# Three small edits in a one-core hybrid attention block: where the norm weights are loaded, how far mixer A's heads are staged apart, how early the last splits are issued

## The chip, the cores and the metric

The kernel runs on one core of a Trainium2 chip. The metric is the device time of one execution in microseconds (us); lower is better. A core has a matrix engine (TensorE, PE in the rows; its weight loads are PEld), a vector engine (VectorE, DVE), a scalar engine (ScalarE, ACT), GpSimd (POOL) and SyncE (SP), which here only issues DMAs. Each engine works its own list of instructions in order and waits on semaphores for the others.

## The reference

One layer of a decoder trunk on x of 256 tokens by 4096 channels, all in float32:

```
h    = rmsnorm(x, norm_g)
proj = h @ w_in                       # 4096 x (26 chunks of 512, and 48 gate columns)
o_a  = dilated attention of 16 heads over q_a, k_a, v_a      (mixer A)
o_b  = compressed / selected / window attention, 16 heads    (mixer B)
y    = concat(rmsnorm(o_a) * silu(z_a), rmsnorm(o_b) * silu(z_b))
x    = rmsnorm(x + y @ w_out, final_g)
```

In mixer A the three patterns of a head act on one 256-token sequence, so the kernel computes one softmax per head with a table of multiplicities (`MULT`) and a table of distances (`DA`).

## The kernel before

Every float32 product is made of three fast products: an operand is split into a rounded part h and a rest l, and `mm3` (lines 98 to 100) adds h·h, h·l and l·h. `split_to` (lines 105 and 106) makes the two parts of a weight tile: ScalarE writes h, then VectorE writes l from it. So each weight tile passes through SyncE's queue (load), ScalarE, VectorE and TensorE, in this order.

The program has four parts. **Part one** streams three weight chunks past x (`run_stream`): `stage_unit` loads weight units `w`, `load_xT` loads the transposed x in pieces `xp`, `split_x` makes `xh` and `xl` = x times the norm weights `g_in`, and `split_unit` makes `wh` and `wl`. Every `xh` reads `g_in`. The first unit is loaded and split in small pieces so that TensorE can begin early; before that TensorE runs 13 dummy products (`warm_up`). **Part two** (`run_pairs`) computes most of the projection by a fast block scheme. **Part three** streams the z chunks and the first output chunk, and between their products the two attentions run: they are generators in a queue `tasks`, and `advance()` takes one step of the first of them, about 1.5 steps per 128 rows of weights. The attention of mixer A is `attend_a`, once for each group of four heads; its three stages per head are `scores` (products `s`, then the softmax numerators `n` on VectorE and ScalarE), `turn` (transposes `pt` of `n`, line 677, and the split `pah`, `pal`) and `values` (products `po`). `pipeline(units, stages, at)` runs them in rounds, where stage f of unit j comes in round j + at. `mixer_done` loads the stored z tiles (`sz`), applies silu and multiplies them into the output. **Part four** is `run_pairs` for the output projection and then two chunks of 256 columns. The last chunk is held back: its pieces are split into `ehl` and `eh`/`el` by `split_held` and kept, since all products for the first 128 tokens are done before those for the second 128.

A tile scheduler orders each engine's list in parts one and three by its own estimate; parts two and four stand as written. Each DMA that SyncE or ScalarE issues takes one of eight DMA semaphores in turn (DMAHW0 to 7), and an issue waits until the DMA that had this semaphore eight issues ago has landed.

Of the kernel before, what the change touches and what calls it, by code (L numbers as in the profile page):

```python
# [83 lines left out]
def hybrid_trunk(ctx: ExitStack, tc: tile.TileContext, a: dict):  # L84
    nc = tc.nc
# [32 lines left out]
    g_in = cst.tile([P, KT], F32, name="g_in")  # L118
# [13 lines left out]
    def load_xT(piece):  # L132
        q, half = divmod(piece, 2)
        if half == 0:
            xh.append(big.tile([P, QK, SEQ], F32R, name=f"xh{q}", tag="x", bufs=8))
            xl.append(big.tile([P, QK, SEQ], F32R, name=f"xl{q}", tag="x", bufs=8))
        t = x_raw[piece] = room["o"].tile([P, G4, SEQ], F32, name="xp", tag="o", bufs=8)
        if piece == 0:
            nc.gpsimd.dma_start(g_in, a["norm_g"])
            for j, e in ((0, 1), (1, 2), (2, 4)):  # L140
                nc.sync.dma_start(t[:, j:e], a["xT"][piece, :, j:e])
        elif piece == 1:
            for j in range(0, G4, 2):
                nc.sync.dma_start(t[:, j : j + 2], a["xT"][piece, :, j : j + 2])
        else:
            nc.sync.dma_start(t, a["xT"][piece])
# [10 lines left out]
    def load_x_nat(i):  # L157
        m, q = divmod(i, 4)
        t = x_nat[i] = room["work"].tile([P, DM // 4], F32, name="xn", tag="xn", bufs=4)
        nc.sync.dma_start(t, a["x"][m * P : (m + 1) * P, q * DM // 4 : (q + 1) * DM // 4])  # L160
# [109 lines left out]
            square_x(2 * (u - 8) + half)  # L270
        splitted[u, half] = (h, l)

    LOOK = 2
    def split_held(u, half, i):

        t = staged[u]
        n, width = 4, units[u][1]
        if i < 5:
            hl = room["held"].tile([P, 2, n, width], F32R, name="ehl", tag="ehl", bufs=5)
            h, l = hl[:, 0], hl[:, 1]  # L280
        else:
            h = room["split"].tile([P, n, width], F32R, name="eh", tag="wh")
            l = room["split"].tile([P, n, width], F32R, name="el", tag="wl")
        split_to(h, l, t[:, half * n : (half + 1) * n])
        splitted[u, half] = (h, l)
# [13 lines left out]
    def run_stream(begin=None, last=False, ordered=None):  # L299
        subs = [(u, s) for u in range(len(units)) for s in range(2)]  # L300
        n_st = n_sp = 0
        credit = 0.0
        ps = None
        first = room["first"]
        held_chunk = len(chunks) - 1 if last else None
        for i, (u, s) in enumerate(subs):
            while True:
                if n_st < len(units) and n_st <= u + (2 if i else 0):
                    if first and n_st < 8:
                        load_xT(n_st)  # L310
                    stage_unit(n_st)
                    if first and 8 <= n_st < 12:
                        load_x_nat(2 * (n_st - 8))
                        load_x_nat(2 * (n_st - 8) + 1)
                    n_st += 1
                    if first and n_st == 1:
                        warm_up()
                    if first and n_st == 6:
                        early_loads()
                elif n_sp < len(subs) and n_sp <= i + LOOK and subs[n_sp][0] < n_st:  # L320
                    if units[subs[n_sp][0]][4] == held_chunk:
                        if n_sp == len(subs) - 8:
                            open_held()
                        split_held(*subs[n_sp], n_sp - len(subs) + 8)
                    else:
                        split_unit(*subs[n_sp])
                    n_sp += 1
                elif i == 0 and n_st < 3:
                    if first:
                        load_xT(n_st)  # L330
                    stage_unit(n_st)
                    n_st += 1
                else:
                    break
            if i == 0 and begin:
                begin()
                if ordered:
                    ordered.close()
            src, width, k0, n, c = units[u]
            n //= 2  # L340
            _, lhs, done, before, pace = chunks[c]
            if k0 == 0 and s == 0:
                if before:
                    before()
                ps = [room["acc"].tile([P, CW], F32, name="acc", tag="acc") for _ in range(NT)]
            if c == held_chunk:
                wh, wl = splitted[u, s]
                for j in range(n):
                    h, l = lhs(k0 + n * s + j, 0)
                    mm3(ps[0][:, :width], h, l, wh[:, j], wl[:, j], start=(i == len(subs) - 8 and j == 0),  # L350
                        stop=(i == len(subs) - 1 and j == n - 1))
                for _ in range(2):
                    advance()
                continue
            wh, wl = splitted.pop((u, s))
            for j in range(n):
                k = k0 + n * s + j
                for m in range(NT):
                    h, l = lhs(k, m)
                    mm3(ps[m][:, :width], h, l, wh[:, j], wl[:, j], start=(k == 0), stop=(k == KT - 1))  # L360
                if k == KT - 1:
                    done(ps)
                if (c, k) in hooks:
                    hooks[c, k]()
                credit = min(credit + pace * width / CW, 2.0)
                while credit >= 1.0 and tasks:
                    credit -= 1.0
                    advance()
        if not last:
            return  # L370

        while tasks:
            advance()
        done(ps, 0)
        for i, (u, s) in enumerate(subs[-8:]):
            wh, wl = splitted.pop((u, s))
            k0, n = units[u][2:4]
            n //= 2
            for j in range(n):
                h, l = lhs(k0 + n * s + j, 1)  # L380
                mm3(ps[1][:, :width], h, l, wh[:, j], wl[:, j], start=(i == 0 and j == 0), stop=(i == 7 and j == n - 1))
        done(ps, 1)
# [241 lines left out]
    def pipeline(units, stages, at):  # L624

        for t in range(len(units) + at[-1]):
            for f, d in reversed(list(zip(stages, at))):
                if 0 <= t - d < len(units):
                    f(units[t - d])
            yield  # L630
            yield

    def attend_a(hg):
# [59 lines left out]
                nc.scalar.activation(t[:, m], po[:, m], AF.Copy, scale=rden[:, m : m + 1])  # L693
            nc.vector.tensor_add(o_at("a", head * HD, HD), t[:, :, 0], t[:, :, 1])

        yield from pipeline(range(4), [scores, turn, values], [0, 1, 2])
        square_sums("a", hg)

    def square_sums(which, hg):
# [520 lines left out]
    def early_loads():  # L1220
        nc.sync.dma_start(ident, a["consts"][:, N_CONST - P :])
        nc.sync.dma_start(g_out, a["out_g"])
# [231 lines left out]
```

## Time and profile before

| | |
|---|---|
| median of three runs | 1630.84 us (1629.99 to 1634.46) |
| profiled execution, its own time | 1628.41 us |
| its span, first to last instruction | 1626.6 us |
| TensorE busy | 1605.9 us, 99% of the span |
| VectorE, ScalarE busy | 1369.2 us, 995.5 us |
| mean granted TensorE clock | 0.998 of full speed |

The span is what the trace shows; the profiled execution's own time has 1.8 us more around it. TensorE is busy nearly all the time, so what can be read from the trace is above all where it is not.

### The profile page before, as it was taken

The page shows a single profiled execution, that of the slowest core. Times are in us where ns is not written, and L with a number is a line of the kernel's source. Part 1 is how long each engine was busy: PE and PEld are TensorE (multiplying, and loading weights), DVE is VectorE, ACT ScalarE, POOL GpSimd, SP SyncE. Part 2 cuts the span into 40 slices and gives each one's busy share as a digit, 9 for nine tenths or more (in the row PEclk, how much of TensorE's full clock was granted, in tenths as well). Part 3 has the DMA queues.
Part 4 walks back from the last instruction along what each step waited for, and adds up shares of the span by engine and source line. Part 5 has one row for each costly group of instructions (what it writes and reads, how often), then busy time and mean ns, then how long its engine had stood idle before and what let it go on. Part 6 is the DMA issues. An engine that isn't in the chain of part 4 may idle for free.

```text
span 1626.6 us, 20699 instructions
## 1 busy us (share of the span) xinstructions
PE 1605.9 (99%) x7685; PEld 1324.3 (81%) x7685; DVE 1369.2 (84%) x1596; ACT 995.5 (61%) x1242; POOL 143.3 (9%) x197
## 2 busy tenths in 40 slices
PE   8999999999999999999999999999999999999997
PEld 6998888888888888888887777888888888888896
DVE  7679989898999898989878788888777769989884
ACT  7755656565656565656546666766667655656553
POOL 0000212020212021202000000000000000212110
PEclk9999999999999999999999999999999999999999
DMA  8776888888888788978787464643355456878874
GB/s 326 275 249 209 259 264 256 256 260 264 255 269 263 247 265 259 269 242 269 242 333 300 157 213 170 227 140 127 135 187 182 170 200 212 261 250 257 279 300 166
DMA packets 104452, 384.86 MB, mean 237 GB/s; under 512 B 12368, under 2 KB 13024, under 8 KB 92960
## 3 DMA queue, kind: packets, MB, share of 16 engines
q1 hardware_dynamic: 81648, 332.40, 57.9%
q0 software_dynamic: 22272, 50.10, 13.8%
q8 instruction: 60, 0.98, 0.2%
q10 hardware_dynamic: 432, 1.05, 0.2%
q14 instruction: 40, 0.33, 0.1%
HBM read 334.69 MB, written 50.91 MB: 237 GB/s over the span
## 4 chain that ended last, share of the span: by engine, by line
PE 84%; DVE 7%; DMA 4%; issue 2%; ACT 2%; POOL 0%; SPq 0%; ACTq 0%; POOLq 0%; DVEq 0%
PE p L99 15%; PE p L100 15%; PE p L98 15%; PE acc L99 8%; PE acc L100 8%; PE acc L98 8%; PE e L100 2%; PE e L99 2%; PE e L98 2%; DVE bf L440 1%; DMA bw<-in_w_in 1%; DVE bf L439 1%; PE ph L872 1%; PE pt L1053 1%; DVE bt L433 1%
## 5 line engine op out<-in xcount | busy, mean ns | idle before, releaser
L106 DVE TENSOR_TENSOR wl<-w,wh 128x1024 fp32r<-128x1024 f32 (+2 forms) x178 | 207.7, 1171 | 87.5 <-ACT wh L105 86.9
L98 PE MATMUL acc<-wh,xh 128*128 128x512 f32 (+2 forms) x640 | 242.3, 379 | 3.4 <-ACT wh L105 3.4
L105 ACT ACTIVATE wh<-w 128x1024 fp32r<-128x1024 f32 (+2 forms) x178 | 180.3, 1017 | 105.1 <-PE acc L100 88.7
L440 DVE TENSOR_TENSOR bf<-bt,bf 128x2048 fp32r<-128x2048 f32 x106 | 242.1, 2284 | 0.0
L99 PE MATMUL acc<-wl,xh 128*128 128x512 f32 (+2 forms) x640 | 240.4, 376 | 1.0 <-DVE wl L106 1.0
L100 PE MATMUL acc<-wh,xl 128*128 128x512 f32 (+2 forms) x640 | 239.9, 375 | 0.0
L106 DVE TENSOR_TENSOR bp<-bw,bp 128x2048 fp32r<-128x2048 f32 x72 | 164.8, 2288 | 70.5 <-ACT bp L105 70.5
L435 ACT ACTIVATE bf<-bt 128x1024 fp32r<-128x1024 f32 x106 | 112.3, 1060 | 168.8 <-DVE bt L433 168.8
L432 ACT ACTIVATE bf<-bw 128x1536 fp32r<-128x1536 f32 x106 | 157.6, 1487 | 66.5 <-DMA bw<-in_w_in 38.9
L105 ACT ACTIVATE bp<-bw 128x2048 fp32r<-128x2048 f32 x72 | 137.5, 1910 | 96.6 <-PE e L100 77.7
L439 DVE TENSOR_TENSOR bf<-bw,bf 128x1536 fp32r<-128x1536 f32 x106 | 185.6, 1751 | 0.0
L433 DVE TENSOR_TENSOR bt<-bw 128x1024 f32<-128x1024 f32 x106 | 129.4, 1221 | 12.2 <-DMA bw<-in_w_in 7.6
L98 PEld LDWEIGHTS acc<-wh,xh 128*128 128x128 f32 x640 | 120.5, 188 | 21.9 <-ACT wh L105 3.9
L438 ACT ACTIVATE bf<-bt 128x1024 fp32r<-128x1024 f32 x106 | 112.7, 1063 | 41.8 <-DVE bt L437 39.6
L99 PEld LDWEIGHTS acc<-wl,xh 128*128 128x128 f32 x640 | 120.7, 189 | 19.6 <-DVE wl L106 2.3
L100 PEld LDWEIGHTS acc<-wh,xl 128*128 128x128 f32 x640 | 120.3, 188 | 19.0
L98 PE MATMUL p<-bp,xh 128*128 128x512 f32 x324 | 126.0, 389 | 0.0
L99 PE MATMUL p<-bp,xh 128*128 128x512 f32 x324 | 126.0, 389 | 0.0
L100 PE MATMUL p<-bp,xl 128*128 128x512 f32 x324 | 126.0, 389 | 0.0
L99 PE MATMUL p<-bf,sum 128*128 128x512 f32 x320 | 124.7, 390 | 0.2 <-DVE bf L440 0.2
L98 PE MATMUL p<-bf,sum 128*128 128x512 f32 x320 | 124.7, 390 | 0.0
L100 PE MATMUL p<-bf,sum 128*128 128x512 f32 x320 | 124.6, 389 | 0.0
(328 smaller groups left out, 3381.5 us busy)
## 6 DMA issues: line engine op xcount, KB each, us to landing
bw<-in_w_in SPq DMA_DIRECT2D x288, 512.0 KB, 6.4
w<-in_w_in SPq DMA_DIRECT2D x60, 1024.0 KB, 4.9
bw<-in_w_out SPq DMA_DIRECT2D x96, 512.0 KB, 5.3
w<-in_w_out SPq DMA_DIRECT2D x16, 1024.0 KB, 4.8
scr_q<-parts POOLq DMA_DIRECT2D x30, 256.0 KB, 7.8
scr_k<-parts POOLq DMA_DIRECT2D x30, 256.0 KB, 7.9
scr_v<-parts POOLq DMA_DIRECT2D x30, 256.0 KB, 7.9
scr_qb<-parts POOLq DMA_DIRECT2D x30, 256.0 KB, 8.0
```

The costliest lines, as they stand in the source:

```text
L98: nc.tensor.matmul(out, lh, rh, start=start, stop=False)
L99: nc.tensor.matmul(out, lh, rl, start=False, stop=False)
L100: nc.tensor.matmul(out, ll, rh, start=False, stop=stop)
L105: nc.scalar.activation(h, src, AF.Copy)
L106: nc.vector.tensor_sub(l, src, h.bitcast(F32))
L432: nc.scalar.activation(h[:, :3], w[:, B22:], AF.Copy)
L433: nc.vector.tensor_tensor(t[:, T3 : T1 + 1], w[:, B22 : B11 + 1], w[:, B12 : B12 + 1].to_broadcast([P, 2, CW]), op=OP.subtract)
L435: nc.scalar.activation(h[:, 3:5], t[:, T3 : T1 + 1], AF.Copy)
L438: nc.scalar.activation(h[:, 5:], t[:, T2:], AF.Copy)
L439: nc.vector.tensor_sub(l[:, :3], w[:, B22:], h[:, :3].bitcast(F32))
L440: nc.vector.tensor_sub(l[:, 3:], t, h[:, 3:].bitcast(F32))
L872: nc.tensor.matmul(ph, both, w[:, :, j], start=l == 0, stop=l == CBL - 1)
```

## The change

Three edits, with no instruction added or removed on any compute engine. `g_in` is loaded from SyncE's queue behind the first piece of x, where GpSimd issued that load before. Mixer A's stages stand two rounds apart, so that three heads are between `scores` and `values` at a time, and a group of four heads takes eight rounds for six. The pieces of the last chunk may be split four pieces ahead of the product in work; all others still two.

```diff
         if piece == 0:
-            nc.gpsimd.dma_start(g_in, a["norm_g"])
             for j, e in ((0, 1), (1, 2), (2, 4)):
                 nc.sync.dma_start(t[:, j:e], a["xT"][piece, :, j:e])
+                if j == 0:
+                    nc.sync.dma_start(g_in, a["norm_g"])
...
-    LOOK = 2
+    LOOK, LOOK_HELD = 2, 4
...
+        held = len(subs) - 8 if last else len(subs)
...
-                elif n_sp < len(subs) and n_sp <= i + LOOK and subs[n_sp][0] < n_st:
+                elif n_sp < len(subs) and n_sp <= i + (LOOK_HELD if n_sp >= held else LOOK) and subs[n_sp][0] < n_st:
...
-        yield from pipeline(range(4), [scores, turn, values], [0, 1, 2])
+        yield from pipeline(range(4), [scores, turn, values], [0, 2, 4])
```

SyncE's list at the start of the program, with the semaphore that an issue waits for, before:

```order
L141 DMA xp<-in_xT 128x256 x2
L141 DMA xp<-in_xT 128x512
L144 DMA xp<-in_xT 128x512 x2
L252 DMA w<-in_w_in 128x1024 [waits DMAHW0_49]
L252 DMA w<-in_w_in 128x1024 [waits DMAHW1_49]
```

and of the change, where line numbers are one higher:

```order
L140 DMA xp<-in_xT 128x256
L142 DMA g_in<-in_norm_g 128x32
L140 DMA xp<-in_xT 128x256
L140 DMA xp<-in_xT 128x512
L145 DMA xp<-in_xT 128x512
L145 DMA xp<-in_xT 128x512 [waits DMAHW0_49]
L253 DMA w<-in_w_in 128x1024 [waits DMAHW1_49]
L253 DMA w<-in_w_in 128x1024 [waits DMAHW2_49]
```

The load of `g_in` takes a place in the queue and a semaphore, so the second half of x's next piece, which waited for nothing, now waits for the first weight piece (DMAHW0).

TensorE's list in the first group of mixer A's heads, at the first `turn`, before (`acc` are the z chunk's products, `pt<-ident,n` the transposes, `s` the next head's scores, `po` the values):

```order
L100 MATMUL acc<-wh,xl_169 128x512
L677 MATMUL pt<-ident,n 128x128
L98 MATMUL s<-kaT,qaTh 128x128
L677 MATMUL pt<-ident,n 128x128 x2
L99 MATMUL s<-kaT,qaTh 128x128
L100 MATMUL s<-kaT,qaTl 128x128
L98 MATMUL s<-kaT,qaTh 128x256
L99 MATMUL s<-kaT,qaTh 128x256
L100 MATMUL s<-kaT,qaTl 128x256
L98 MATMUL acc<-wh,xh_168 128x512
L689 MATMUL po<-va,pah 128x256
L99 MATMUL acc<-wl,xh_168 128x512
```

and of the change, at the same place:

```order
L100 MATMUL acc<-wh,xl_169 128x512
L680 MATMUL pt<-ident,n 128x128 x3
L98 MATMUL s<-kaT,qaTh 128x128
L99 MATMUL s<-kaT,qaTh 128x128
L100 MATMUL s<-kaT,qaTl 128x128
L98 MATMUL s<-kaT,qaTh 128x256
L99 MATMUL s<-kaT,qaTh 128x256
L100 MATMUL s<-kaT,qaTl 128x256
L98 MATMUL acc<-wh,xh_168 128x512
```

The three transposes stand together, with one more head's scores behind the `n` that they read; the first `po` comes 26 rows later.

ScalarE's list in the last two chunks (`wh` the last pieces of the chunk before, `ehl` and `eh` those of the last; `junk,ssr` sums of squares of output chunks that were loaded back), before:

```order
L105 ACTIVATE wh<-w 128x1024
L1131 ACTIVATE junk,ssr<-r_12162 128x512
L1131 ACTIVATE junk,ssr<-r_12164 128x512
L105 ACTIVATE ehl<-w 128x1024
L1131 ACTIVATE junk,ssr<-r_12162 128x512
L1131 ACTIVATE junk,ssr<-r_12164 128x512
L105 ACTIVATE ehl<-w 128x1024
L1131 ACTIVATE junk,ssr<-r_12210 128x512
L1131 ACTIVATE junk,ssr<-r_12232 128x512
L1131 ACTIVATE junk,ssr<-r_12210 128x256
L1131 ACTIVATE junk,ssr<-r_12232 128x256
L105 ACTIVATE ehl<-w 128x1024 x3
```

and of the change:

```order
L105 ACTIVATE wh<-w 128x1024
L105 ACTIVATE ehl<-w 128x1024 x2
L1134 ACTIVATE junk,ssr<-r_12162 128x512
L1134 ACTIVATE junk,ssr<-r_12164 128x512
L105 ACTIVATE ehl<-w 128x1024
L1134 ACTIVATE junk,ssr<-r_12162 128x512
L1134 ACTIVATE junk,ssr<-r_12164 128x512
L105 ACTIVATE ehl<-w 128x1024
L1134 ACTIVATE junk,ssr<-r_12210 128x512
L1134 ACTIVATE junk,ssr<-r_12232 128x512
L1134 ACTIVATE junk,ssr<-r_12210 128x256
L1134 ACTIVATE junk,ssr<-r_12232 128x256
```

Four `ehl` now stand ahead of the two sums of 256 columns, which wait for the end of the chunk before; two stood there. VectorE's list moves in the same way.

## Rows read from the trace of the kernel before

**Rows 1.** The page, busy time, share of the span and instructions of TensorE.

```profile
PE 1605.9 (99%) x7685; PEld 1324.3 (81%) x7685; DVE 1369.2 (84%) x1596; ACT 995.5 (61%) x1242; POOL 143.3 (9%) x197
```

**Rows 2.** Waits of TensorE over the span: us in total, times, longest.

```profile
PE acc L98 <- ACT wh L105: 3.4, 1, 3.4
...
PE pt L598 <- DVE fetched L567: 1.1, 2, 0.7
PE acc L99 <- DVE wl L106: 1.0, 2, 0.8
PE acc L99 <- DVE ehl L106: 0.9, 1, 0.9
PE acc L98 <- ACT ehl L105: 0.7, 1, 0.7
PE pt L677 <- DVE n L667: 0.5, 3, 0.2
```

**Rows 3.** Timeline of ScalarE, first 16 us: start, us, instruction, idle before, releaser.

```profile
7.89 0.51 ACT L108 ACTIVATE xh<-xp,g_in 128x256 fp32r<-128x256 f32 x1 [4.25 <-DMA g_in<-in_norm_g]
...
12.39 1.04 ACT L105 ACTIVATE wh<-w 128x1024 fp32r<-128x1024 f32 x1
```

**Rows 4.** Timeline of TensorE, first 16 us.

```profile
8.97 0.74 PE L98 MATMUL acc<-wh,xh 128*128 128x512 f32 x2 [3.37 <-ACT wh L105]
...
15.19 0.39 PE L99 MATMUL acc<-wl,xh 128*128 128x512 f32 x1
```

**Rows 5.** Timeline of VectorE, first 16 us.

```profile
13.47 1.23 DVE L106 TENSOR_TENSOR wl<-w,wh 128x1024 fp32r<-128x1024 f32 x1
```

**Rows 6.** DMA issues of the first 5 us: count, size, median us to landing.

```profile
xp<-in_xT SPq DMA_DIRECT2D x2, 128.0 KB, 5.1
g_in<-in_norm_g POOLq DMA_DIRECT2D x1, 16.0 KB, 6.6
```

**Rows 7.** Timeline of SyncE's issues, first 40 us.

```profile
0.74 1.34 SPq L141 DMA_DIRECT2D xp<-in_xT  x3
...
5.73 0.84 SPq L252 DMA_DIRECT2D w<-in_w_in  x2
...
20.87 0.43 SPq L1221 DMA_DIRECT2D ident<-in_consts  x1
21.35 0.43 SPq L1222 DMA_DIRECT2D g_out<-in_out_g  x1
```

**Rows 8.** DMA issues at 5.72 to 6.0 us, as in rows 6.

```profile
w<-in_w_in SPq DMA_DIRECT2D x1, 512.0 KB, 6.4
```

**Rows 9.** DMA issues at 20.8 to 21.9 us, as in rows 6.

```profile
ident<-in_consts SPq DMA_DIRECT2D x1, 64.0 KB, 8.0
g_out<-in_out_g SPq DMA_DIRECT2D x1, 16.0 KB, 7.8
```

**Rows 10.** Chain that ended last, in order of time, 955 to 1222 us.

```profile
964.21 6.99 DMA fetched<-scr_k
...
1210.09 7.28 DMA sz<-scr_zb
```

**Rows 11.** Timeline of ScalarE, 1210 to 1221 us.

```profile
1217.45 0.63 ACT L749 ACTIVATE sz<-sz 128x512 f32<-128x512 f32 x1 [4.66 <-DMA sz<-scr_zb]
```

**Rows 12.** Timeline of TensorE, 1586 to 1598 us.

```profile
1591.09 0.28 PE L98 MATMUL acc<-ehl,yh 128*128 128x256 f32 x1
1591.21 0.28 PE L99 MATMUL acc<-ehl,yh 128*128 128x256 f32 x1
...
1594.86 0.38 PE L98 MATMUL acc<-ehl,yh 128*128 128x256 f32 x1 [0.73 <-ACT ehl L105]
1596.12 0.39 PE L99 MATMUL acc<-ehl,yh 128*128 128x256 f32 x1 [0.88 <-DVE ehl L106]
```

**Rows 13.** Timeline of VectorE, 1582 to 1600 us.

```profile
1589.09 1.22 DVE L106 TENSOR_TENSOR ehl<-w,ehl 128x1024 fp32r<-128x1024 f32 x1 [0.26 <-ACT ehl L105]
...
1594.84 3.50 DVE L106 TENSOR_TENSOR ehl<-w,ehl 128x1024 fp32r<-128x1024 f32 x3 [0.52 <-ACT ehl L105]
```

## The prediction

> **What bounds the kernel now.** I read the page first: TensorE is busy 1605.9 us of the span, 99% [rows 1]. The change adds no product and removes none, so it can give back only time in which TensorE stands idle, and can cost only by making more of it. The next view is therefore the list of TensorE's waits [rows 2]: 3.4 us before the first real product, for the first split weights; 1.1 us for attention inputs that are fetched and scaled (two waits); 0.5 us for softmax numerators before their transposes (three waits); 1.0 us for weight rests, VectorE's `wl` (two waits); 0.9 and 0.7 us for the held pieces `ehl` of the last chunk. Beside these stands the end of the program, after the last product, which no edit touches. The first, the second to fourth in part, and the last pair are where the three edits act; I take them one by one.
>
> **Edit 1, the norm weights.** ScalarE sits idle 4.25 us until `g_in` lands and begins the first `xh` at 7.89; TensorE's first product follows at 8.97, after 3.37 us of idle time [rows 3, 4]. The first piece of x is issued at 0.74 and such pieces take 5.1 us in the middle, so x is there at about 5.8; `g_in`, from GpSimd, takes 6.6 us and comes last [rows 6, 7]. In the change `g_in` is SyncE's second issue. The three issues of the first group take 1.34 us together, 0.45 each [rows 7], so it goes out at about 1.2, and with the 5.1 us of its neighbours it lands near 6.3, some 1.6 us earlier. If nothing else were late, the first product would come 1.6 us earlier.
>
> What is late next is the weights. The second unit's first half is issued at 5.73 and lands 6.4 us later, at 12.1; ScalarE splits it at 12.39 [rows 3, 7, 8]. So ScalarE can come forward by only 0.3 us there, however early it began. VectorE makes the rest from 13.47 to 14.70, and TensorE takes it at 15.19, 0.5 us later [rows 4, 5]. TensorE can thus be ahead by 0.3 + 0.5 = 0.8 us at that product and no more; the rest of the 1.6 us is spent waiting between 8 and 15 us, in small pieces. Does that load itself move? At 5.73 SyncE's queue today gets past its wait for the first weight piece and issues it; in the change half a piece of x stands there first, behind the same wait, so the load goes out one issue later, at about 6.2. But it takes 6.4 us to land where the first piece took 5.1, so it stands in line behind others, and 0.45 us later in the line's end need not be later out of it. What `g_in` adds is its own transfer. The nearest row is a load of the same shape in the same queue, `g_out`: issued 0.48 us behind `ident` at 21.35, landing in 7.8 us against 8.0, so 0.2 to 0.3 us behind it [rows 7, 9]. I take 0.2 off: **−0.6 us**. Bounds: −1.6 if the weights come earlier too, and 0 if the queue's delay of one issue (0.45) and the 0.3 of transfer both count, which leaves the 0.8 empty.
>
> The Trainium skill (DMA: Bandwidth & Descriptors, Specifications and Measured) speaks against this edit: it asks for at least 512 B for each descriptor, and its table gives 0.68 us to a 4 KB transfer and 0.95 to one of 64 KB, small ones being bound by their descriptors; `g_in` has 128 rows of 128 B. By an estimate from that page, about 0.75 us between the two, the pieces behind `g_in` would all be 0.75 us late and edit 1 would be worth nothing; the row of `g_out` says 0.2 to 0.3 and decides until the run.
>
> GpSimd loses an issue at the start; nothing is queued behind it there. Once TensorE is ahead it stays ahead: no wait for splits stands in the list between 16 us and the middle of the program except two short ones, and these hang on buffers that TensorE's own products release, so they move with it.
>
> **Edit 2, mixer A.** Product for product the same work; sixteen more rounds' steps (two rounds, two steps each, four groups), so that everything behind mixer A comes later in the stream of z products. What goes: a transpose now reads numerators that were made two rounds before. The three waits for `n`, 0.5 us, should vanish [rows 2]. The waits for fetched inputs, 1.1 us, come from a fetch that is issued late and takes 7.0 us [rows 10]; in the new order the next group's fetch is issued while the last heads are still at `values`, and more than 50 products (each 0.23 us) lie between it and its transposes, 12 us. I expect them gone. Late in mixer B's gating ScalarE stands 4.66 us for a third stored z tile, whose load takes 7.3 us, and TensorE then waits 0.3 of the 1.0 us in the row for `wl` [rows 2, 10, 11]; since mixer A now ends later, that third tile is stored in time to be gated with mixer A, and only two are left. In sum 0.5 + 1.1 + 0.3 = 1.9 us. What may come: the values of the last two heads stand only six products apart (1.4 us), and their one result buffer has to be emptied between them by ScalarE; and four z tiles are gated after mixer A where three were. The nearest row for such a new wait is the 0.17 us of one wait for `n` (0.5 in three) [rows 2]; I take two of these, 0.4: **−1.5 us**. Bounds: −1.9, and +1.0 (the fetch waits stay, 0.8 goes, and new ones cost what the row for `wl` has, its 1.0 and its longest 0.8 again).
>
> If mixer A's cover were gone, the price would be seen at the end of the stream: before, 144 z products lie between mixer B's last transpose and the first transpose of the gated output, now 66, which is 15 us. The gates that these transposes read are mixer A's, long done.
>
> **Edit 3, the last chunk.** Its first product is at 1591.09, and twelve products of 0.12 us make a piece, 1.44 us [rows 12]. Pieces three onwards are split only after the chunk before is finished, so TensorE waits 0.73 and 0.88 us at the third [rows 12]. In the change four pieces are ready first; the fifth is wanted at 1591.09 + 4 × 1.44 = 1596.85. But two more rests on VectorE, 1.14 us each (3.50 for three that overlap a little), now stand ahead of the finish of the chunk before. VectorE idles 0.26 and 0.52 us in that stretch [rows 13], so the fifth rest starts at about 1594.84 + 2.3 − 0.8 = 1596.3 and is done at 1597.5: TensorE waits 0.5 us there, and later pieces come each 1.14 us against a need of 1.44. The gain is 1.6 − 0.5 = 1.1; since ScalarE's part may be late too I take **−1.0 us**. Bounds: −1.6 (no wait), −0.5 (a wait of 1.1). It is nothing if the fifth piece's weights land after 1596, and earlier splits free their load buffer earlier, so I exclude a loss.
>
> **Sum.** −0.6 − 1.5 − 1.0 = −3.1 us, against the profiled execution's 1628.41: 1625.3. The median of the runs shown lies 2.4 us higher, at 1630.84, so the forecast for a median is **1627.7 us**, 0.19% less. From no change a measurement of this kernel can tell about 0.3%, 4.9 us; the forecast is below that.
>
> **The rivals.**
> 1. All covers hold and the weights follow `g_in` forward: −1.6 − 1.9 − 1.6 = −5.1, 1625.7. For it: every wait named is on the path of an engine that is 99% busy. Against it: the second unit's landing at 12.1 [rows 8] and VectorE's load at the end.
> 2. Edits 1 and 2 only move their waits: edit 1 worth nothing, edit 2 the 0.5 us of `n` alone, edit 3 1.0: −1.5, 1629.3. For it: the fetch and the first loads are DMA-bound, and a DMA does not get faster by another order. Against: the counted distance of 12 us for the fetch. The page on DMA would have edit 1 end here, with its 0.75 us of delay.
> 3. Slower: at the end of mixer B both z tiles are loaded in one go, behind weight loads in SyncE's queue, and ScalarE holds two silu pairs in its list ahead of weight splits. Today 4.66 us of such waiting costs TensorE 0.3 us [rows 2, 11], so about 4.4 us are covered. If ScalarE waited for one whole load of 7.3 us [rows 10] and then for part of the other, 10 us in all, TensorE would lose 5.6 us: with edits 1 and 3 (−1.6) that is +4.0, 1634.8. It decides from a wait of 4.4 + 1.6 = 6 us upwards, and passes +0.3% from 11 us. Against it: one pair of tiles fewer than today.
> 4. The order does not do what it says, since a scheduler has the last word: edit 2 worth nothing, −1.6, 1629.2. The rows of the order show that it does move.
>
> **How the numbers follow.** Chances: the forecast 0.58 (its own range 1626 to 1629.5), rival 1 0.13, rival 2 0.17, rival 3 0.07, rival 4 0.05. Faster by over 0.3% needs −4.9: most of rival 1 and the lower edge of the forecast, since the runs before lie 4.5 us apart: 0.20. Slower by over 0.3%: rival 3 in its worse half and the same scatter: 0.07. Within: 0.73. The range takes in rival 1 below with a little scatter, 1624.3, and rivals 2 and 4 above with the same, 1631.3; rival 3 stays outside.
>
> **What would show it.** Edit 1: `g_in` lands at 6 to 6.5 us, the first product is at 7.1 to 7.6, but the product that was at 15.19 is at 14.4 to 14.8. Edit 2: no TensorE wait for `n` or for fetched inputs, no 4.66 us wait of ScalarE late in mixer B. Edit 3: the waits at the third held piece gone, one of about 0.5 us at the fifth. I would be wrong if a weight load at the start landed later than today, or if TensorE waited for `po` or for splits in mixer A's stretch.

## The result and the profile after

The changed kernel takes 1623.94 us (median of 6 runs, 1622.32 to 1625.37); the kernel before, beside it, 1631.95 (6 runs, 1629.99 to 1634.46). The ratio is 0.9949 (95% interval 0.9936 to 0.9962): 8.0 us less, where 3.1 were forecast, and 0.4 us under the range. The profiled execution takes 1622.32 us with a span of 1620.5, so the two profiles lie 6.1 us apart. One profiled execution, of the first run with cut values further below, took 2683 us at a granted clock of 0.556; no time and no reading here uses it.

The page's row for TensorE in the changed kernel, against [rows 1]:

```profile
PE 1601.9 (99%) x7685; PEld 1326.4 (82%) x7685; DVE 1368.8 (84%) x1596; ACT 994.6 (61%) x1242; POOL 142.6 (9%) x196
```

The same 7685 products show 4.0 us less busy time. The prediction said that only idle time could be given back. TensorE's waits in the changed kernel, as in [rows 2]:

```profile
PE s L98 <- DVE pal L106: 2.8, 4, 1.1
PE acc L99 <- DVE wl L106: 1.3, 2, 0.7
...
PE acc L99 <- DVE ehl L106: 0.7, 1, 0.7
PE acc L98 <- ACT wh L105: 0.6, 1, 0.6
PE p L99 <- DVE bf L443: 0.5, 1, 0.5
```

The waits for `n` and `fetched` are gone, as forecast, but four new ones are there, 2.8 us: scores that wait for `pal`. By this list part three should have got worse. To see where the time went I took marks in both traces: the same z or output product, timed in each. The first is the product on the 64th weight piece, the second that on the 138th; between them lie both attentions. Before:

```profile
914.26 0.48 PE L98 MATMUL acc<-wh,xh 128*128 128x512 f32 x1
...
1222.99 0.39 PE L98 MATMUL acc<-wh,xh 128*128 128x512 f32 x1
```

and after:

```profile
912.65 0.48 PE L98 MATMUL acc<-wh,xh 128*128 128x512 f32 x1
...
1217.16 0.48 PE L98 MATMUL acc<-wh,xh 128*128 128x512 f32 x1
```

So this stretch, "the stretch" from here on, takes 304.5 us where it took 308.7. The other marks are the 18th piece (51.51 before, 50.80 after), the first held product (1591.09, 1585.38) and the last product (1616.13, 1609.26). In order of time the pair differs by −0.7 (start), −0.9 (51 us to the 64th piece, where no edit acts; this part varies by 3 us over the profiles below), −4.2 (the stretch), +0.1, −1.2 (the last chunk), +0.8 (behind the last product; this tail is 10.4 to 10.7 or 11.3 us long over the profiles, with and without each edit): −6.1. The edits' own parts were forecast as −0.6, −1.5 and −1.0 and came out as −0.7, −4.2 and −1.2. One term is off.

The start of the changed kernel, in TensorE's timeline against [rows 4]:

```profile
7.16 0.73 PE L98 MATMUL acc<-wh,xh 128*128 128x512 f32 x2 [0.60 <-ACT wh L105]
14.39 0.50 PE L99 MATMUL acc<-wl,xh 128*128 128x512 f32 x1 [0.61 <-DVE wl L106]
```

The DMA issues of its first 5 us, and one at 5.7 us, against [rows 6, 8]:

```profile
g_in<-in_norm_g SPq DMA_DIRECT2D x1, 16.0 KB, 4.8
...
w<-in_w_in SPq DMA_DIRECT2D x1, 512.0 KB, 6.3
```

Nearly everything here goes as worked out: `g_in`, issued at 1.19, lands at 5.99 (6.3 was said), the first product is at 7.16 (7.1 to 7.6), and the product that was at 15.19 is at 14.39, ahead by the 0.8 us that the weights allow, with a new wait of 0.61 us in front. The weight load goes out at 5.70, not at 6.2: it stands one issue further back, but the first weights, whose landing is waited for, were there at 5.31 where they had come at 5.71. One load is late: the piece of x right behind `g_in` is issued 0.47 us later than before and lands at 7.47 for 6.77, and ScalarE waits 0.38 us for it. The piece behind that one lands earlier, at 8.82 for 9.56.

At the end one wait of 0.70 us stands for 1.61 before, against [rows 12]:

```profile
1592.13 0.39 PE L99 MATMUL acc<-ehl,yh 128*128 128x256 f32 x1 [0.70 <-DVE ehl L106]
```

### The profile page after: what moved, and what is told of

It is laid out like the page before. It is cut to its first block, busy times and chain, and to the rows that moved or that the text cites. A ratio compares the mean times of both kernels' runs of the same rounds, so it can differ in the third digit from the quotient of the medians.

```text
span 1620.5 us, 20719 instructions
## 1 busy us (share of the span) xinstructions
PE 1601.9 (99%) x7685; PEld 1326.4 (82%) x7685; DVE 1368.8 (84%) x1596; ACT 994.6 (61%) x1242; POOL 142.6 (9%) x196
## 4 chain that ended last, share of the span: by engine, by line
PE 89%; DVE 6%; issue 2%; DMA 2%; ACT 1%; SPq 0%; ACTq 0%; POOLq 0%; POOL 0%; DVEq 0%
PE p L99 16%; PE p L100 16%; PE p L98 16%; PE acc L99 9%; PE acc L100 9%; PE acc L98 9%; PE e L100 2%; PE e L98 2%; PE e L99 2%; PE ph L875 1%; DVE wl L106 1%; PE pt L1056 1%; DVE bf L443 1%; DMA w<-in_w_in 1%; DVE bp L106 1%
## 5 line engine op out<-in xcount | busy, mean ns | idle before, releaser
L436 DVE TENSOR_TENSOR bt<-bw 128x1024 f32<-128x1024 f32 x106 | 129.5, 1222 | 12.6 <-DMA bw<-in_w_in 7.0
```

The source lines that it names most:

```text
L436: nc.vector.tensor_tensor(t[:, T3 : T1 + 1], w[:, B22 : B11 + 1], w[:, B12 : B12 + 1].to_broadcast([P, 2, CW]), op=OP.subtract)
```

## Where the stretch lost its time: the waits of the weight loads

Each product has two rows in a trace: the load of its stationary operand (PEld) and the product itself (PE). A product's end is modelled; a row lasts 0.39 us where the next starts 0.23 us later. The list of PE's waits begins to count at that modelled end, so a stop of up to 0.16 us behind a long product is not in it. The load has no such cover. The waits of the weight loads in the stretch, kernel before (us in total, times, longest):

```profile
PEld po L689 <- ACT pah L105: 4.3, 15, 0.4
PEld po L98 <- ACT pbh L105: 2.5, 9, 0.4
PEld pt L677 <- DVE n L667: 2.5, 9, 0.4
...
PEld pt L598 <- PE acc L100: 1.9, 2, 1.1
PEld pt L677 <- PE acc L100: 1.5, 4, 0.5
...
PEld po L690 <- DVE pal L106: 0.9, 5, 0.2
```

and the changed kernel:

```profile
PEld s L98 <- DVE pal L106: 3.7, 4, 1.3
PEld po L98 <- ACT pbh L105: 2.6, 9, 0.4
PEld po L99 <- DVE pbl L106: 1.7, 8, 0.3
PEld s L99 <- DVE kaT L106: 1.7, 4, 0.4
```

Before, 15 of 16 heads had their first value product wait for `pah` at its weight load: 4.3 us in a row that TensorE's own list does not hold at all. The two rows of transposes (`pt`) that name PE are waits for VectorE as well: in all six cases the `n` or `fetched` that the transpose reads was finished 0.07 to 0.12 us before the load began (at 1009.06 and 1009.18, for example). In the changed kernel no load waits for `pah` or `n`. Mixer B's rows (`pbh`, `pbl`) stay. One such wait in the kernel before, in PE's timeline:

```profile
926.95 0.40 PE L100 MATMUL acc<-wh,xl 128*128 128x512 f32 x1
927.34 0.39 PE L689 MATMUL po<-va,pah 128*128 128x256 f32 x1
927.56 0.40 PE L98 MATMUL acc<-wh,xh 128*128 128x512 f32 x1
```

and in PEld's:

```profile
927.34 0.19 PEld L689 LDWEIGHTS po<-va,pah 128*128 128x128 f32 x1 [0.31 <-ACT pah L105]
```

PE shows no wait, yet 0.61 us pass from one z product to the next, of which 0.23 are the first one's own: the value product took 0.38 us. Elsewhere in the same kernel a lone value product whose load had nothing to wait for:

```profile
950.66 0.39 PE L100 MATMUL acc<-wh,xl 128*128 128x512 f32 x1
950.88 0.28 PE L689 MATMUL po<-va,pah 128*128 128x256 f32 x1
951.00 0.40 PE L98 MATMUL acc<-wh,xh 128*128 128x512 f32 x1
```

This one took 0.34 − 0.23 = 0.11 us, so 0.27 us were lost above: 0.16 behind the z product, where its modelled end covers them, and 0.11 in the value product's own row, 0.39 us for 0.28. Of the 16 lone value products of the kernel before, the two whose loads stood idle for 0.04 and 0.16 us took 0.11 us each, and the 14 whose loads waited 0.21 to 0.44 us took 0.25 to 0.51. The Trainium skill (Perfetto Trace Analysis, Identifying the Most-Contended Engine) warns that the busy share of matmuls is no measure of how near a kernel is to its limit, because they are pipelined, and asks for the share of the peak rate that the products reach and for the busy share of the weight loads instead. Here the busy shares were 99% and 81% [rows 1], and the warning holds; the share of the loads itself rose to 82% and gives no size, which only the list of their waits does.

That these hidden waits are what the stretch lost is **theory A**. Two more had to be told apart from it. **Theory B**: the order itself changed; before, the scheduler had put mixer A's transposes and values singly between z products, and after they stand in whole groups (the rows of the order show both), so short products among long ones may cost time by themselves, waits or not. **Theory C**, for the 1.9 us that the medians show beyond the profiles: edit 1 also ends an idle time of TensorE behind which its clock falls.

## The experiments

All times are medians; each ratio is to the kernel before on the same chip. The stretch is that of the one profiled execution of each run.

| kernel | us | ratio, 95% interval | stretch, us |
|---|---|---|---|
| edit 1 alone | 1630.45 | 0.9986 (0.9978 to 0.9995) | 310.4 |
| edit 2 alone | 1626.36 | 0.9962 (0.9949 to 0.9976) | 304.3 |
| edit 3 alone | 1629.87 | 0.9988 (0.9979 to 0.9997) | 310.4 |
| distances 0, 1, 3 | 1630.10 | 0.9992 (0.9983 to 1.0001) | 308.2 |
| distances 0, 2, 3 | 1627.33 | 0.9975 (0.9966 to 0.9984) | 305.9 |
| edit 2, values cut in two | 1628.23 | 0.9986 (0.9977 to 0.9995) | 308.7 |
| before, longer dummy work | 1630.70 | 0.9998 (0.9989 to 1.0006) | 312.0 |
| changed, shorter dummy work | 1624.54 | 0.9962 (0.9950 to 0.9975) | 304.7 |
| edits 2 and 3 | 1625.63 | 0.9970 (0.9959 to 0.9982) | 304.8 |
| edits 2 and 3, longer dummy work | 1624.54 | 0.9963 (0.9950 to 0.9975) | 307.1 |
| edits 1 and 2 | 1624.68 | 0.9966 (0.9954 to 0.9979) | 305.8 |
| changed, second and third time | 1622.40, 1623.50 | 0.9951, 0.9958 | 304.3, 305.4 |
| changed, scores first, twice | 1620.37, 1620.51 | 0.9933, 0.9935 | 303.2, 301.7 |

**The edits one by one.** Edit 1 alone is the first hunk of the change, edit 2 alone the last, and edit 3 alone those between them, on the splits.

> Edit 1 alone. If the parts are independent: TensorE's first real product near 7.2 us, the product that was at 15.19 at about 14.4, ahead of before by 0.7 us at 50 us and by 1.5 us at 848 us, as in the changed kernel; nothing gained after that, so the time is 0.7 to 1.5 us below before, and the waits for pah, n and pal on the weight loads stay (4.3, 2.5 and 0.9 us). Rival: the lead at the start lets part three run differently too (weights land earlier against the attention), and then part three itself gains 1 us or more of the 4.1 here already.

> Edit 2 alone. Theory A (hidden waits: the weight loads in front of a product stood waiting for pah, n and pal, up to 0.4 us each, where the list of TensorE's own waits shows nothing because the end of the product before is modelled later than the next start) and theory B (short products put singly among the long z products cost TensorE time by themselves, waits or not) both want part three shorter by about 4 us and no gain elsewhere: 4 us below before. In the weight loads' list the rows for pah, n and pal go from 7.7 us to nearly 0 and one for s on pal of 3 to 4 us comes. If part three is shorter by only 1.5 us, the gain of the changed kernel came from the edits together and both fall.

> Edit 3 alone. By the prediction's working: the two waits of 0.73 and 0.88 us at the third held piece go, one of 0.5 to 0.8 comes at a later piece, 0.8 to 1.1 us below before, all of it after 1590 us. Rival: it is a share of the gain only because TensorE arrived earlier in the changed kernel; alone, weights land early enough for all eight pieces and no wait is left, 1.6 us below before.

The gain of part three is edit 2's, and it is there in full without the others: stretch 304.3 us, loads' row for `s` on `pal` 3.6 us, none for `pah` or `n`. By the medians edit 2 is worth 5.9 us, edits 1 and 3 1.8 and 2.4, with intervals of 1.4 to 2.2 us either way (together 10.1 for the whole change's 8.0, within these intervals). Edit 1 alone has its 18th piece 0.9 us earlier and gains nothing in the stretch, so its rival falls; edit 3 alone takes 23.8 us from its first held product to its last for 25.0 and has one wait left, of 0.6 us, so its rival falls too. What I had not expected is the stretch in edits 1 and 3, 310.4 us. TensorE's waits for fetched inputs in the profile of edit 1 alone and, further below, of the kernel before with longer dummy work:

```profile
PE pt L599 <- DVE fetched L568: 2.3, 2, 1.9
```

```profile
PE pt L598 <- DVE fetched L567: 3.9, 3, 2.1
```

Where the profile of before had 1.1 us [rows 2], these have 2.3 and 3.9, and that of edit 3 alone 2.5. No profile with edit 2's distances has this wait, so by an estimate from these four profiles (2.4 us on average) edit 2 is worth over a microsecond more in an average execution than in the profiled pair. Of 81 timed executions of the kernel before, only two were faster than its profiled one.

**Are the groups or the waits the cost?** Two other distances, and edit 2 with the values cut in two:

```diff
-        yield from pipeline(range(4), [scores, turn, values], [0, 1, 2])
+        yield from pipeline(range(4), [scores, turn, values], [0, 1, 3])
```

(and `[0, 2, 3]` in the other)

```diff
             for m, blocks in enumerate([[(0, 0)], [(P, 0), (2 * P, 1)]]):
+                if m:
+                    yield
...
-        yield from pipeline(range(4), [scores, turn, values], [0, 1, 2])
+        for t in range(8):
+            if t > 3:
+                yield from values(t - 4)
+            else:
+                yield
+            if 2 <= t < 6:
+                turn(t - 2)
+            if t < 4:
+                scores(t)
+            yield
```

> Edit 2 with the distances 0, 1, 3: the transposes come one round behind the scores as before, the values two rounds behind the transposes. In the order nearly all of the splitting of groups of before stays (one transpose alone, one value product alone, in 14 of 16 heads). Theory A: the waits for n stay (2.5 us on weight loads), those for pah and pal (4.3 and 0.9) shrink as far as these stand ready two rounds later; the stretch of part three from the 64th to the 138th weight piece, 308.7 us before and 304.4 with edit 2, shortens by about what these rows lose. Theory B: the groups stay split, so it is no shorter than 308 us, whatever the rows for pah and pal do.

> Edit 2 with the distances 0, 2, 3: the transposes two rounds behind the scores, the values one round behind the transposes as before. Theory A: the waits for n on the weight loads go (2.5 us, and 1.5 us booked on the z product ahead), those for pah stay (4.3 us before); the stretch from the 64th to the 138th weight piece comes out near 306 us. Theory B by its fragments: about half of the heads have their value products split, so also near 306 us; it is told from A by where the excess stands: A at rows with a wait, B at split groups without one.

> Edit 2 alone, and each head's six value products cut in two: the first two stand singly between z products, at least three and mostly six z products ahead of the other four, which are issued one step later. Nothing that they read is later than in edit 2 alone. Theory A: being apart costs nothing, so the time is within 1 us of edit 2 alone. Theory B: a lone product among z products cost 0.22 us more than its columns in the trace of before (0.117 before it and 0.105 behind it), so 16 heads cost 3.5 us and nearly all of edit 2's gain is lost. If the wait of the scores for pal changes, that is read from its own row and taken out of the comparison.

> Edit 2 alone with each head's values cut in two by z products, again, for a trace at the full clock. Theory A: the stretch from the 64th to the 138th weight piece is within 1 us of edit 2 alone (304.3 us) unless a row of waits has grown, and then by that row. Theory B: 16 lone pairs at 0.22 us make it 307.8 us without any row of waits to show for it.

The first run with cut values took 1628.34 us (0.9979, 0.9968 to 0.9989). With distances 0, 1, 3 the stretch is hardly shorter, and the waits of the loads say why:

```profile
PEld po L689 <- ACT pah L105: 2.6, 9, 0.3
PEld pt L677 <- DVE n L667: 2.6, 8, 0.6
...
PEld po L690 <- DVE pal L106: 1.7, 7, 0.3
```

The row for `pah` is 1.7 us shorter, that for `pal` 0.8 longer. This alone fits both theories. With distances 0, 2, 3 the stretch came out as expected, 305.9 us, but not row by row: `n` fell to 1.4 us of the loads' waits, and `pah`, which was to stay at 4.3, to 0.6, while 3.1 us came to stand at `pal`. The cut values, though, came out 4.4 us longer in the stretch than edit 2 alone, against A's "within 1 us unless a row of waits has grown". Rows have: TensorE's waits there, and those of its loads:

```profile
PE pt L677 <- DVE n L667: 4.1, 5, 1.7
```

```profile
PEld pt L677 <- issue: 4.4, 3, 2.1
...
PEld po L691 <- ACT ot L695: 2.3, 9, 0.4
PEld pt L677 <- DVE n L667: 1.2, 4, 0.4
```

My edit had moved the transposes, and they now waited for `n`; the total decides nothing. The single groups do. In PE's timeline of that kernel a lone pair between z products:

```profile
934.22 0.40 PE L100 MATMUL acc<-wh,xl 128*128 128x512 f32 x1
934.45 0.28 PE L691 MATMUL po<-va,pah 128*128 128x256 f32 x1
934.57 0.28 PE L692 MATMUL po<-va,pal 128*128 128x256 f32 x1
934.68 0.40 PE L98 MATMUL acc<-wh,xh 128*128 128x512 f32 x1
```

0.46 − 0.23 = 0.23 us for two, 0.12 each, and that although the first one's load waited 0.16 us; a pair at 1034.01, whose load had nothing to wait for, took the same. An unbroken group of six in the changed kernel takes 0.71 us, also 0.12 each, in 15 of 16 heads; in the other, whose load waited 0.28 us, it took 0.83. Theory B's 0.22 us on a lone product is absent where no load waits, and the kernel before has its own cases above. The transposes say the same: in the kernel before, the eight lone ones whose load stood idle for less than 0.12 us took 0.02 to 0.03 us each. B falls.

The same can be counted over all kernels. I added up, from the rows of PEld in the stretch, the idle time ahead of each load beyond 0.12 us (chosen because the remainders then agree best; it is close to the time of one short product):

```
                          stretch   idle of loads   remainder
before                     308.74       12.97         295.77
edit 1 alone               310.44       14.59         295.85
before, longer dummy work  312.03       16.30         295.73
edit 2 alone               304.33        8.64         295.69
changed                    304.50        8.89         295.61
distances 0, 1, 3          308.17       12.84         295.33
distances 0, 2, 3          305.92       10.50         295.42
edit 2, values cut         308.72       11.88         296.84
edits 2 and 3              304.83        9.11         295.72
changed, scores first      301.69        6.83         294.86
```

Stretches that differ by 10 us leave remainders within 1 us of each other but for the cut values, which keep 1.1 us more: at most 0.07 us for each of 16 cuts. By itself the sum does not tell A from B, since a stop of TensorE for any cause is idle time ahead of some load. What does is how these idle times end: in the traces of before and of the changed kernel every one of them, 85 and 49, ends 0.04 to 0.11 us after ScalarE or VectorE has set a semaphore that this load or its product waits for. So the waits of the loads account for edit 2's whole gain, 13.0 − 8.9 = 4.1 us.

**The new wait.** The fourth head's scores want the PSUM buffer of the first transposes, and these are free only when VectorE has made `pal`, behind two weight rests. The changed kernel with a round's scores ahead of its transposes:

```diff
-        yield from pipeline(range(4), [scores, turn, values], [0, 2, 4])
+        yield from pipeline(range(4), [turn, scores, values], [2, 0, 4])
```

> The changed kernel with the scores of a round issued ahead of its transposes. In the changed kernel the fourth head's scores wait 2.8 us in four waits, because their PSUM buffer is that of the first transposes, whose rests pal stand behind two weight rests in VectorE's list. With the scores first they take a buffer that was read a round earlier. If that is the cause: the row for s on pal goes from 2.8 us (3.7 on the weight loads) to under 0.5, and the time is 2 to 3 us below the changed kernel, 0.9930 to 0.9937 of before. Rival: the transposes now need the buffer and wait instead, or VectorE's list is what is late, and the time stays that of the changed kernel, 0.9949.

> The changed kernel again, beside the next one on the same chip: 0.9949 of before, within the interval that was measured (0.9936 to 0.9962); the stretch from the 64th to the 138th weight piece 304.5 us, with the four waits of the scores for pal.

> The changed kernel with a round's scores ahead of its transposes, again, beside the changed kernel. From the trace of its first run the stretch from the 64th to the 138th weight piece is 1.3 us shorter (303.2 for 304.5), of the 2.8 us that its waits for pal had; the times of the two runs differ by 3.5 us. If only the trace's gain is real, it is 1.3 us (0.0008) below the changed kernel here; if the time's is, 3.5 us (0.0022).

TensorE's waits in the stretch, scores first, second profile, and a row of its loads' waits:

```profile
PE po L692 <- ACT ot L696: 0.6, 2, 0.3
```

```profile
PEld po L692 <- ACT ot L696: 1.8, 3, 0.7
```

The 2.8 us are gone (3.7 on the loads), as the cause said; 0.6 us for the values' result buffer came, and here too the loads' list has more, 1.8 us. Beside the changed kernel on one chip it is 1.9 us faster (1620.51 and 1622.40), between the 1.3 and 3.5 us of the first comparison; the stretches differ by 1.3 and 2.6 us. It is the fastest kernel of this study, 0.9933 and 0.9935 of before.

**The clock at the start.** The kernel before with more dummy products, and the changed one with fewer:

```diff
-WARM = 13
+WARM = 21
```

(`WARM = 4` in the other)

> The kernel before with 21 dummy products for 13 at the start, and none of the three edits: TensorE is kept busy until about 8 us and stands idle for at most 1.5 us ahead of the first real product, where it stood 1.9 to 3.4 us in the runs without edit 1. In four of six of those profiles the granted clock fell to 0.5 behind that idle time, for 3 to 6 us, and the 18th weight piece came at 52.9 to 53.8 us; in two it did not fall (51.3 and 51.5). Theory C (edit 1 is worth more than its 0.7 us of earlier data because it ends this idle time and with it the fall of the clock): no fall here, the 18th piece at 51.2 to 51.8, the time 1 to 1.5 us below before. Rival: the fall has nothing to do with the idle time; it comes here too, or the longer dummy work itself makes the first products late, and the time is that of before or above.

> The changed kernel with 4 dummy products for 13, so that TensorE stands idle for about 3 us again ahead of the first real product, while the norm weights still land early. Theory C: the granted clock falls in most executions and these are 1.4 to 2.3 us longer than the changed kernel, and the runs lie further apart. Rival (edit 1 gains by earlier data alone): the time is that of the changed kernel within 0.5 us.

Both inconclusive. With 21 products the clock did not fall and the 18th piece came at 51.69 us, as theory C said, but the execution had 3.9 us of waits for fetched inputs, and the time did not move. With 4 products the time rose by 2.1 us against the changed kernel on the same chip, but the profile shows no fall behind 3.69 us of idle time, and only 1 us lost by the 18th piece (its second unit's weights landed at 12.59 us, later than in any profile with edit 1 and 13 products, 11.59 to 12.30). So the comparison was repeated where edit 2 has taken the noise of the fetch away. Without edit 1 (edits 2 and 3), and that with `WARM = 21`:

```diff
+            nc.gpsimd.dma_start(g_in, a["norm_g"])
             for j, e in ((0, 1), (1, 2), (2, 4)):
                 nc.sync.dma_start(t[:, j:e], a["xT"][piece, :, j:e])
-                if j == 0:
-                    nc.sync.dma_start(g_in, a["norm_g"])
```

> The changed kernel without edit 1 (edits 2 and 3 stay, so the wait for fetched inputs, 1.1 to 3.9 us from profile to profile of the kernels without edit 2, is out of the comparison). If edit 1 is worth its earlier data alone, as the pair of profiles shows (0.7 us at the 18th weight piece), this is 0.7 us above the changed kernel. Theory C: the clock also falls behind the idle time in two of three executions and costs 1.4 to 2.3 us there, so this is 1.7 to 2.2 us above, and its runs lie further apart.

> The kernel of the run before this one (edits 2 and 3 alone) with 21 dummy products for 13, so that TensorE is busy until 8.9 us. Theory C: no fall of the clock, so it is faster than that kernel by 1.0 to 1.5 us and 0.7 to 0.9 us above the changed kernel. If the clock does not matter, it is that kernel's time within 0.4 us.

> The changed kernel, beside the three before on the same chip: 0.9950 of before, as twice measured (0.9949 and 0.9951).

Without edit 1 it is 2.1 us slower than the changed kernel; longer dummy work gives 1.1 of them back. The intervals overlap, and the profile of the longer dummy work has 2.3 us more in the stretch, so this is not shown; the sizes are those of theory C. Windows of TensorE without edit 1 (us, TensorE's busy time and products, granted clock, then DMA):

```profile
8.00:9.00 1.00, 0.10 (x1) 1.00 1.08 395
9.00:10.00 1.00, 1.00 (x3) 0.87 0.95 350
10.00:11.00 1.00, 1.00 (x4) 0.50 1.00 389
...
13.00:14.00 1.00, 1.00 (x5) 0.92 1.02 418
```

and with longer dummy work:

```profile
9.00:10.00 1.00, 0.61 (x2) 1.00 1.02 352
10.00:11.00 1.00, 1.00 (x5) 1.00 1.07 426
```

In the first, TensorE had idled 2.17 us up to 8.90; then the granted clock stood at half (1.2 GHz) for three microseconds, in which a product started every 0.43 us, where it is every 0.23 us at the full clock. In the second the dummy work ended at 7.57, not at 8.9 as expected, so 1.60 us of idle time were left, and the clock stayed up. The 18th piece comes at 52.97 us there, 51.93 with longer dummy work, and 50.4 to 51.1 in the seven profiles with edit 1 and 13 dummy products. The clock fell in five of the seven profiles without edit 1 and with 13 dummy products, and in none of the ten others. That it is the idle time that brings it down is argued from this count and not shown: the profile with 4 dummy products had the longest idle time, 3.69 us, and kept its clock.

**Edit 3 on its own.** The changed kernel without it:

```diff
-    LOOK, LOOK_HELD = 2, 4
+    LOOK = 2
...
-        held = len(subs) - 8 if last else len(subs)
...
-                elif n_sp < len(subs) and n_sp <= i + (LOOK_HELD if n_sp >= held else LOOK) and subs[n_sp][0] < n_st:
+                elif n_sp < len(subs) and n_sp <= i + LOOK and subs[n_sp][0] < n_st:
```

> The changed kernel without edit 3. By the profile of the changed kernel edit 3 takes away 0.9 us of waits: this is 0.9 us above it. By the difference of the single run of edit 3 alone (2.4 us below before, with an interval of 1.5 either way) it could be more; above 1.6 us, all that the two waits have, would need another cause.

It is 1.2 us slower than the changed kernel, and from its first held product to its last product it takes 24.8 us; the changed kernel takes 23.9 in each of its three profiles.

## Why the prediction was wrong

**Edit 1** was right in the profile: 0.7 us for 0.6, by the path that was worked out (the weights, not `g_in`, set the gain). Of the delay of about 0.75 us behind `g_in`, an estimate that the prediction had worked out from the Trainium skill (DMA: Bandwidth & Descriptors, Specifications and Measured), the trace shows this much: the piece of x right behind `g_in` was 0.70 us late, 0.47 of that by its later issue, but the next piece was 0.74 us early, and the half unit issued at 5.70 landed in 6.3 us, the one before in 6.4 [rows 8]. The weights set the gain and were not delayed, so the edit did not end at nothing. What the working left out is the fall of the clock. The profile of before showed 3.37 us of idle time and a clock that stayed up, and I read no more from it; in five of seven profiles with the same start the clock fell, and the 18th piece came another 1.4 to 2.3 us later than in that of before. By the medians edit 1 is worth 1.8 and 2.1 us in its two comparisons, each with 1.4 us or more either way; that the clock makes up the difference to 0.7 is the best account and not shown.

**Edit 2** is where the working failed, at its first sentence: "it can give back only time in which TensorE stands idle", read from the list of TensorE's own waits. That list held 1.9 us for the stretch; the loads' list held `pah`, 4.3 us, and most of `n` (4.0 us, where TensorE's had 0.5). The term was −1.5 and is −4.2 in the pair of profiles. Each mechanism in it was right (numerators two rounds old, the fetch in time, no third z tile late in mixer B), and the new wait that it allowed 0.4 us for came as 2.8 us, at another place than the one named: not the result buffer of the values but the buffers of scores and transposes. It is one of the prediction's own signs of being wrong, a wait of TensorE for splits in mixer A's stretch. The two errors partly cancel, so it is luck that the term was off by no more than 2.7 us. The fetch wait was taken at its 1.1 us, the shortest of four profiles.

**Edit 3** was right: −1.0 forecast, −1.2 in the last chunk of the pair. The one wait left, 0.70 us where 0.5 was said (the prediction's own times, 1597.5 and 1596.85, give 0.6), stands at the 50th held product, the second of the fifth piece, for VectorE's rest, as worked out from VectorE's list; that rest in turn began 0.52 us late, for ScalarE's part of the piece.

**The step from profile to median** added 2.4 us to the forecast as if the scatter of before stayed. A part of it, the fetch wait and the fall of the clock, is what the edits remove: the runs of the changed kernel lie 1621.5 to 1625.4 (16 runs), those of before 1627.7 to 1635.4 (81). That is the best account of the 1.9 us between 6.1 and 8.0; with an interval of 2.1 us either way on the 8.0 it is not shown to the digit.

## What to carry to other kernels

On a TensorE that reads as 99% busy, read the waits of its weight loads too, before pricing a change that makes an operand ready earlier: fifteen waits of 0.2 to 0.4 us were missing from its own list. Staging a short chain two rounds apart for one paid here because its operands came up to 0.4 us after the work of one round was done; but count the buffers of every tile that then lives longer, and issue the taker of a buffer where its last reader is long done. A single profile is one draw: ask which waits in it hang on DMA landings or on the clock, and price a change on those over several profiles.

## What the runs showed of the hardware

Changing between long z products and short ones of another shape costs TensorE nothing measurable: 0.11 to 0.12 us for a 256-column product alone, in a pair or in a group of six. Behind 1.9 to 3.1 us of idle time early in the program the granted clock fell to 0.5 for about 3 to 6 us in five profiles, and it stayed up behind 3.0, 3.4 and 3.7 us in three others, two of them with the same start; what decides is open. A 16 KB load of 128-byte rows landed 4.1 to 4.8 us after its issue from SyncE and 6.4 to 6.8 us after its issue from GpSimd. The load of x right behind it in SyncE's queue was issued 0.47 us later than without it and landed at 7.2 to 8.0 us in the eight profiles with edit 1, at 6.3 to 6.8 in nine without; the next load of x landed earlier, at 8.7 to 9.1 us for 9.3 to 9.8.
